# Retention of one decoder block on Trainium2: two halves of the tokens with a state between them, and the decay moved out of the scores

## The chip, the cores and the metric

The kernel runs on one core of one Trainium2 chip. What is measured is the device time of one launch in microseconds (us). The kernel before was run three times: median 1729.63 us, from 1728.58 to 1733.28. One further execution was profiled; it took 1730.48 us, of which 1728.0 us lie between the first and the last instruction (the span). All rows below come from that execution.

## The reference

One layer of a decoder block on 1024 tokens of width 1024, all in float32: half a SwiGLU feed-forward step (inner width 2816), then a mixer, then another half feed-forward step, with an RMS norm ahead of each and one at the end. The mixer projects the normed tokens into 512 columns for a pooling mixer and into queries, keys, values and gates of four heads of 128 columns each. The pooling mixer (trailing means over 2, 4, 8 and 16 tokens, less the token, times a 128x128 matrix per group) is left alone by the change. The heads compute a retention, which the reference writes in chunks; what it amounts to is

```
q, k = rope(q), rope(k) * 128 ** -0.5
gamma[h] = 1 - 2 ** (-5 - h)                     # h = 0..3
o[n] = sum over m <= n of gamma ** (n - m) * (q[n] . k[m]) * v[m]
o = o * rsqrt(mean(o * o) + 1e-6) * gain         # per token and head
b = silu(g) * o
h = h + concat([pooled, b]) @ w_out
```

The sum over m can be split at any token: what lies before the split goes in through one 128x128 matrix per head, the state, which is the sum of k[m] v[m] with the decay up to the split.

## The kernel before

Activations lie with features on the 128 partitions and tokens along the free axis; 1024 tokens (`T`) are worked on in two halves of 512 (`HT`). Each float32 operand is split into two parts of the matmul's input type: ScalarE (ACT) casts the high part, VectorE (DVE) subtracts it from the original and writes the low part (`split`, L78 to L82). A product is then three matmuls, high by high, low by high, high by low, added up in one accumulator in PSUM (`mm3`, L104 to L109). In a profile row such as `ps<-ph,vh` the first operand streams through the array and the second is the one that was loaded as weights. There are eight PSUM banks, all under one tag (`ps`, L73), handed out in turn; a new tile waits until the bank's last reader is done. Weights and read-backs come through three buffers of one tag (`raw`).

The program has three parts: the first feed-forward step (to about 640 us), the mixer (640 to about 1060), the second feed-forward step. The diff touches the mixer alone. There, four projections of the pool run first, then query, key and gate of head 0 (`heads_proj`), the values of heads 0 and 1 (`proj_v`, for two heads at once), and `pool_out`, whose results go to DRAM (`pool_dram`). In `proj_v` the sums in PSUM are split with a factor per token (`scale_split`, L190 to L195): `rcol` holds the norm of each token in the layout with tokens on partitions. The keys and queries pass through `rope` on the way out of PSUM: DVE makes `e`, ACT and GpSimd (POOL) make `f` (L761 to L765), POOL adds them, and `late` splits the sum.

Then come the steps, one for each head, half of the tokens and block of 128 keys. A score tile has keys on the partitions and up to 512 tokens in the free axis. In the first half of a head there are 4 key blocks, with 512, 384, 256 and 128 tokens (what lies above the diagonal is cut off); in the second half 8 key blocks, with 512 tokens five times, then 384, 256, 128. That is 12 steps a head, 48 in all. For each, `scores` makes the tile of the next step on TensorE (PE), DVE multiplies it by a piece of the decay table of the head (`dec`, 1024 columns, L798), and `split` makes `ph` and `pl`. Then comes the fill, then `values` (keys' values by the tile, into an accumulator that runs over the half). The tiles `ph` and `pl` have two buffers each; `p` shares its two (tag `t0`) with `po` of `pool_out`; `f` and the temporary `rs` of the norm share two others (tag `t1`). `dec` has one buffer, which a DMA of 512 KB fills per head, and which it shares with temporaries of the pool.

The fill is work of PE that does not wait for the scores. For heads 0 to 2 it is the projections of the next head: a generator with 24 pieces, each of 6 matmuls of 512 columns (one 128-deep block, three products, two halves). Two pieces stand in each step. For head 3 it is the first part of the output projection (`w_out`), whose accumulators hold two PSUM banks per block of 128 output columns, while `pool_back` reads the pool's results back from DRAM in eight pieces (DMA, cast, subtract). At the end of a half `close` begins: the square of the accumulator for the norm (`ro`), the gain and gate (`y`, L818), and in the steps i+2, i+3, i+4 the pieces of `rstd` (a sum over the partitions by two matmuls with ones, `root`, a Newton step) and the split into `cat`, the input of `w_out`. After the steps the rest of `w_out` runs, with the residual and the next norm.

No table sets the order: the code is written in the order in which each engine's instructions stand, and each engine runs its own in that order.

Of the kernel before, what the change touches and what calls it, by code (L numbers as in the profile page):

```python
# [9 lines left out]
F32 = mybir.dt.float32  # L10
F32R = mybir.dt.float32r
AF = mybir.ActivationFunctionType
ALU = mybir.AluOpType
# [8 lines left out]
NF = FF // P  # L22
NP = NF // 2
# [28 lines left out]
def block(ctx, tc, a):  # L52
# [73 lines left out]
    def rstd(r, n):  # L126

        w = r.shape[-1]
        hi, lo = short("n0", w, F32R), short("n1", w, F32R)
        split(r, hi, lo)  # L130
        yield
        o = ps(w)
        nc.tensor.matmul(o, ones, hi, start=True, stop=False)
        nc.tensor.matmul(o, ones, lo, start=False, stop=True)
        yield from root(o, r, n)

    def root(o, r, n):

        w = r.shape[-1]
        v = short("n2", w)  # L140
        nc.vector.tensor_scalar(out=v, in0=o, scalar1=1.0 / n, scalar2=EPS, op0=ALU.mult, op1=ALU.add)
        yield
        nc.scalar.activation(r, v, AF.Abs_reciprocal_sqrt)
        yield
        s = short("rs", w)
        nc.vector.tensor_tensor(out=s, in0=r, in1=r, op=ALU.mult)  # L146
        nc.vector.tensor_tensor(out=s, in0=s, in1=v, op=ALU.mult)
        nc.vector.tensor_scalar(out=s, in0=s, scalar1=-0.5, scalar2=1.5, op0=ALU.mult, op1=ALU.add)
        nc.vector.tensor_tensor(out=r, in0=r, in1=s, op=ALU.mult)
# [546 lines left out]
    sinr = pool.tile([P, T], F32, name="sinr")  # L696
    r_dram = dp.tile([1, T], F32, name="r_dram", tag="r_dram")
# [32 lines left out]
    def proj_v(pair):  # L730
# [3 lines left out]
        for t0 in (0, 4):  # L734
# [9 lines left out]
            for i, o in enumerate(acc):  # L744
                tb = t0 + i
                scale_split(o, rcol[:, tb:tb + 1], vh[:, tb], vl[:, tb])
# [36 lines left out]
    acc, parts, decs = {}, {}, {}  # L783

    def scores(hd, h, j):

        if hd not in decs:
            decs[hd] = pool.tile([P, T], F32, name="dec", tag="dec", bufs=1)
            nc.sync.dma_start(out=decs[hd], in_=a["decay"][hd])
        q, k = qs[hd][h], ks[hd][0]  # L790
        at = max(0, j * P - h * HT)
        n, off = HT - at, h * HT + at - j * P
        s = ps(n)
        mm3(s, cut(k, slice(None), slice(j * P, j * P + P)), cut(q, slice(None), slice(at, HT)), True, True)
        e = pool.tile([P, HT], F32, name="p", tag="t0", bufs=2)[:, :n]
        ph = pool.tile([P, HT], F32R, name="ph", tag="ph", bufs=2)[:, :n]
        pl = pool.tile([P, HT], F32R, name="pl", tag="pl", bufs=2)[:, :n]
        nc.vector.tensor_tensor(out=e, in0=s, in1=decs[hd][:, off:off + n], op=ALU.mult)  # L798
        split(e, ph, pl)
        parts[hd, h, j] = (ph, pl), at  # L800

    def values(hd, h, j):
        if j == 0:
            acc[hd, h] = ps()
        p, at = parts.pop((hd, h, j))
        vs = slice(hd % 2 * P, hd % 2 * P + P)
        mm3(acc[hd, h][:, at:], cut(vs_of[hd // 2], slice(None), j, vs), p, j == 0, j == 4 * h + 3)

    def close(hd, h):
# [7 lines left out]
        y, ro = (pool.tile([P, HT], F32, name=n, tag=n, bufs=b) for n, b in (("y", 1), ("ro", 2)))  # L817
        nc.scalar.activation(ro, o, AF.Square)  # L818
# [3 lines left out]
        yield from rstd(ro, P)  # L822
# [3 lines left out]
    cats = {}  # L826
# [53 lines left out]
    for n, gi in enumerate((3, 2, 1, 0)):  # L880
# [8 lines left out]
        if n == 1:  # L889
# [5 lines left out]
            nc.sync.dma_start(out=rcol, in_=r_dram.rearrange("o (c p) -> p (o c)", p=P))  # L895
    qs, ks, sgs, vs_of, late_ks = {}, {}, {}, {}, []
# [53 lines left out]
    steps = [(hd, h, j) for hd in range(HEADS) for h in range(2) for j in range(4 * (h + 1))]  # L950
# [4 lines left out]
    for i, (hd, h, j) in enumerate(steps):  # L955
# [10 lines left out]
        n = 2 if hd < 3 or i % 12 < 2 else 1  # L966
# [9 lines left out]
        if j == 4 * h + 3:  # L976
# [116 lines left out]
def _tables(np):  # L1093
# [9 lines left out]
    rel = np.arange(T)[None, :] - np.arange(P)[:, None]  # L1103
    dec = np.exp(lg[:, None, None] * np.maximum(rel, 0)[None]) * (rel >= 0)[None] * float(P) ** -0.5
    invc = np.tile((1.0 / np.arange(1, 17)).astype(f)[None], (P, 1))
    return cos2, sin2, dec.astype(f), invc


def _arrange(np, i):
# [13 lines left out]
    def w2s(w):  # L1123
# [11 lines left out]
    cos2, sin2, dec, invc = _tables(np)  # L1135
# [15 lines left out]
        "decay": c(dec),  # L1151
# [21 lines left out]
```

## Time and profile before

The table shows the profiled execution cut at the borders of the work, by the windows of the trace.

| stretch, us | what runs | length, us | PE busy, us | granted clock |
|---|---|---|---|---|
| 0 to 640 | first feed-forward step | 640 | 625.36 | 0.97 to 1.00 |
| 640 to 776 | projections of pool, head 0, values | 136 | 135.41 | 1.00 |
| 776 to 990 | the steps of the retention | 214 | 203.80 | 0.98 |
| 990 to 1060 | rest of `w_out` | 70 | 70.00 | 1.00 |
| 1060 to 1728 | second feed-forward step | 668 | 650.16 | 0.99 |
| profiled execution | 1730.48 us, span 1728.0 | | 1684.7 (97%) | 0.99 |

The page puts PE at 1684.7 us busy (97% of the span), DVE at 1291.0 (75%), ACT at 847.9 (49%), POOL at 258.3 (15%). PE's matmuls overlap at their ends in the records, so a row's mean duration is longer than the distance from one start to the next. The granted clock is given as a share of full speed (2.4 GHz); the other level is 1.2 GHz, a share of 0.50.

### The profile page before, as it was taken

How to read it: one execution, taken by the hardware profiler on the slowest of the kernel's cores; microseconds unless marked ns; L12 is line 12 of the kernel's file. 1: busy time of each engine (PE TensorE's matmuls, PEld its weight loads, DVE VectorE, ACT ScalarE, POOL GpSimd, SP SyncE). 2: the span in 40 equal slices, each digit the busy share in tenths (PEclk: the TensorE clock that was granted, in tenths of full speed). 3: DMA queues.
4: the chain of work that ended last, by engine and by line, in shares of the span. 5: the costliest groups of instructions: out<-in, count | busy, mean ns of one | idle time of the engine just before them, and what ended most of it. 6: DMA issues, size and time to landing. Idle time of an engine off the chain costs nothing.

```text
span 1728.0 us, 21236 instructions
## 1 busy us (share of the span) xinstructions
PE 1684.7 (97%) x7646; PEld 1395.8 (81%) x7646; DVE 1291.0 (75%) x1933; ACT 847.9 (49%) x1379; POOL 258.3 (15%) x228
## 2 busy tenths in 40 slices
PE   8989999999999999999999999989999999999997
PEld 6778888888888888897887788867888888888886
DVE  4978877787778766836657764878777877788667
ACT  5745545554555443344544443655455545554433
POOL 1022012201220101212202020121022102220200
PEclk9999999999999999999999999999999999999998
DMA  9275467546754653231121254373577457744732
GB/s 280 104 152 107 100 153 153 116 97 148 152 121 106 140 176 116 74 106 36 49 79 60 82 196 152 98 146 88 126 147 144 102 120 147 155 98 113 159 134 98
DMA packets 109210, 212.96 MB, mean 123 GB/s; under 512 B 10929, under 2 KB 12977, under 8 KB 109106
## 3 DMA queue, kind: packets, MB, share of 16 engines
q0 software_dynamic: 45280, 97.53, 29.4%
q1 hardware_dynamic: 62994, 113.54, 20.4%
q8 instruction: 59, 0.97, 0.2%
q10 hardware_dynamic: 832, 0.55, 0.1%
q14 instruction: 45, 0.37, 0.1%
HBM read 114.07 MB, written 94.38 MB: 121 GB/s over the span
## 4 chain that ended last, share of the span: by engine, by line
PE 78%; DVE 8%; issue 7%; DMA 3%; ACT 2%; POOL 1%; SPq 0%; DVEq 0%; ACTq 0%; POOLq 0%
PE ps L109 26%; PE ps L108 26%; PE ps L107 26%; DMA raw<-in_f_w 1%; POOL f L764 1%; DMA raw<-pool_dram 1%; DVE t L82 1%; POOL e L765 1%; DVE pl L82 1%; DMA h_dram<-o 1%; DVE wl L82 1%; DVE rs L146 1%; DVE S L247 0%; DVE y L1080 0%; DVE xs L309 0%
## 5 line engine op out<-in xcount | busy, mean ns | idle before, releaser
L502 POOL DMA_DIRECT2D h_dram<-o x144 | 175.2, 1287 | 867.1 <-DVE o L499 860.9
L81 ACT CAST wh<-raw 128x512 fp32r<-128x512 f32 x275 | 170.4, 620 | 210.7 <-PE ps L109 110.4
L107 PE MATMUL ps<-p,wh 128*128 128x512 f32 x648 | 253.9, 392 | 8.2 <-ACT wh L81 4.9
L82 DVE TENSOR_TENSOR wl<-raw,wh 128x512 fp32r<-128x512 f32 x275 | 186.5, 688 | 95.8 <-ACT wh L81 95.5
L108 PE MATMUL ps<-p,wl 128*128 128x512 f32 x648 | 253.5, 392 | 0.0
L109 PE MATMUL ps<-p,wh 128*128 128x512 f32 x648 | 252.4, 391 | 0.0
L107 PE MATMUL ps<-t,wh 128*128 128x512 f32 x608 | 238.0, 391 | 6.8 <-DVE c L462 5.6
L108 PE MATMUL ps<-t,wl 128*128 128x512 f32 x608 | 237.5, 391 | 0.0
L109 PE MATMUL ps<-t,wh 128*128 128x512 f32 x608 | 237.3, 390 | 0.0
L81 ACT CAST wh<-S 128x512 fp32r<-128x512 f32 x224 | 138.7, 620 | 200.8 <-PE ps L109 132.4
L497 ACT ACTIVATE o<-ps 128x512 f32<-128x512 f32 x288 | 162.4, 598 | 13.0 <-DMA h_dram<-o 4.9
L82 DVE TENSOR_TENSOR wl<-S,wh 128x512 fp32r<-128x512 f32 x224 | 152.3, 686 | 18.4 <-ACT wh L81 17.7
L247 DVE TENSOR_TENSOR S<-raw 128x512 f32<-128x512 f32 x112 | 77.1, 689 | 105.8 <-DMA raw<-in_f_w 60.1
L499 DVE SCALAR_TENSOR_TENSOR o<-ps,o 128x512 f32<-128x512 f32 x216 | 134.0, 681 | 26.1 <-DMA h_dram<-o 17.9
L107 PEld LDWEIGHTS ps<-p,wh 128*128 128x128 f32 x648 | 122.4, 189 | 34.8 <-ACT wh L81 4.9
L108 PEld LDWEIGHTS ps<-p,wl 128*128 128x128 f32 x648 | 122.5, 189 | 25.9 <-DVE wl L82 0.6
L109 PEld LDWEIGHTS ps<-p,wh 128*128 128x128 f32 x648 | 122.4, 189 | 25.5
L107 PEld LDWEIGHTS ps<-t,wh 128*128 128x128 f32 x608 | 114.6, 189 | 32.4 <-DVE c L462 6.4
L109 PEld LDWEIGHTS ps<-t,wh 128*128 128x128 f32 x608 | 114.7, 189 | 24.0
L108 PEld LDWEIGHTS ps<-t,wl 128*128 128x128 f32 x608 | 114.7, 189 | 23.7
L107 PE MATMUL ps<-gt,wh 128*128 128x512 f32 x288 | 112.7, 393 | 0.4 <-ACT o L497 0.4
L108 PE MATMUL ps<-gt,wl 128*128 128x512 f32 x288 | 112.7, 391 | 0.0
(197 smaller groups left out, 3296.3 us busy)
## 6 DMA issues: line engine op xcount, KB each, us to landing
h_dram<-o POOLq DMA_DIRECT2D x144, 512.0 KB, 10.3
raw<-in_f_w SPq DMA_DIRECT2D x176, 256.0 KB, 4.6
raw<-in_f_w2s SPq DMA_DIRECT2D x72, 256.0 KB, 4.7
raw<-in_w_t SPq DMA_DIRECT2D x32, 256.0 KB, 2.7
raw<-in_w_o SPq DMA_DIRECT2D x22, 256.0 KB, 2.9
h_dram<-x SPq DMA_DIRECT2D x8, 512.0 KB, 5.3
raw<-in_f_w2c SPq DMA_DIRECT2D x16, 256.0 KB, 2.9
y<-h_dram SPq DMA_DIRECT2D x16, 256.0 KB, 4.0
```

The source lines that it names most:

```text
L81: nc.scalar.copy(hi, src)
L82: nc.vector.tensor_tensor(out=lo, in0=src, in1=hi.bitcast(F32), op=ALU.subtract)
L107: nc.tensor.matmul(out, lh, rh, start=start, stop=False, skip_group_check=chained)
L108: nc.tensor.matmul(out, ll, rh, start=False, stop=False, skip_group_check=chained)
L109: nc.tensor.matmul(out, lh, rl, start=False, stop=stop, skip_group_check=chained)
L146: nc.vector.tensor_tensor(out=s, in0=r, in1=r, op=ALU.mult)
L247: nc.vector.tensor_tensor(out=self.raw[n, out], in0=self.raw[n, x], in1=self.raw[n, y], op=ALU.add)
L497: nc.scalar.activation(x, o, AF.Copy, scale=half)
L499: nc.vector.scalar_tensor_tensor(out=x, in0=o, scalar=half, in1=x, op0=ALU.mult, op1=ALU.add)
L502: nc.gpsimd.dma_start(out=to, in_=out[q][j // 2], accum_op=ALU.add)
L764: nc.gpsimd.tensor_tensor(out=f, in0=f, in1=sinr[:, sl], op=ALU.mult)
L765: nc.gpsimd.tensor_tensor(out=e, in0=e, in1=f, op=ALU.add)
```

## The change

The decay gamma^(n-m) is taken apart. With n and m in the same half of 512 tokens it is gamma^(511-m') / gamma^(511-n'), where m' and n' count inside of the half. The factor of the key's token (and 128^-0.5) goes into the values when they leave PSUM: `gam` holds it for each head and token, `vscale` is its product with `rcol`, and `proj_v` now scales each head's 128 columns apart. The factor of the token n is not divided out: the sums are too small by it, and the norm of the head that follows removes it, if its 1e-6 is scaled by the factor's square. So `rstd` and `root` take a tile `ep` of 512 columns per head (256 KB by DMA) in place of the constant. A score tile then needs only the causal mask, and only in its first 128 columns, where the diagonal block lies: DVE multiplies those by a 128x128 mask, and the other columns are split straight from PSUM.

The second half of a head no longer runs over the first half's keys. Instead the keys of the first half are turned by a matmul with an identity (`turn`, 4 matmuls of 128 columns for the high part in the first step of a head and 4 for the low part in the second), cast by ACT into `kt`, and multiplied with the values over all four blocks (`summed`, 12 matmuls of 128 columns, in the fourth step). The result, times gamma^512, is split into `st`, and three matmuls of 512 columns (state by queries) open the accumulator of the second half. A head has 8 steps now in place of 12, 32 in all. The 24 pieces of fill stand 4, 3, 3, 3, 4, 3, 3, 3 to a step until they run out; in head 3 there are 2 pieces of `w_out` and 2 read-backs of the pool in a step until they run out.

The diff, cut to its core:

```diff
+DECAY = [(1.0 - 2.0 ** (-5 - i)) ** (T // 2) for i in range(4)]
...
-    def rstd(r, n):
+    def rstd(r, n, eps=EPS):
...
-        nc.vector.tensor_scalar(out=v, in0=o, scalar1=1.0 / n, scalar2=EPS, op0=ALU.mult, op1=ALU.add)
+        if eps is EPS:
+            nc.vector.tensor_scalar(out=v, in0=o, scalar1=1.0 / n, scalar2=EPS, op0=ALU.mult, op1=ALU.add)
+        else:
+            nc.vector.scalar_tensor_tensor(out=v, in0=o, scalar=1.0 / n, in1=eps, op0=ALU.mult, op1=ALU.add)
...
+    gam = pool.tile([P, HEADS, NK], F32, name="gam")
+    vscale = pool.tile([P, HEADS, NK], F32, name="vscale")
+    mask = pool.tile([P, P], F32, name="mask")
+    eye = pool.tile([P, P], F32R, name="eye")
+    nc.scalar.dma_start(out=gam, in_=a["gam"])
+    nc.scalar.dma_start(out=mask, in_=a["mask"][0])
+    raw_eye = pool.tile([P, P], F32, name="raw_eye")
+    nc.scalar.dma_start(out=raw_eye, in_=a["mask"][1])
+    nc.scalar.copy(eye, raw_eye)
...
-                scale_split(o, rcol[:, tb:tb + 1], vh[:, tb], vl[:, tb])
+                for c in range(2):
+                    hs = slice(c * P, c * P + P)
+                    scale_split(o[:, hs], vscale[:, 2 * pair + c, tb:tb + 1], vh[:, tb, hs], vl[:, tb, hs])
...
-    acc, parts, decs = {}, {}, {}
+    acc, parts, keyt, state = {}, {}, {}, {}
     def scores(hd, h, j):
-        if hd not in decs:
-            decs[hd] = pool.tile([P, T], F32, name="dec", tag="dec", bufs=1)
-            nc.sync.dma_start(out=decs[hd], in_=a["decay"][hd])
         q, k = qs[hd][h], ks[hd][0]
-        at = max(0, j * P - h * HT)
-        n, off = HT - at, h * HT + at - j * P
+        at = j * P
+        n = HT - at
         s = ps(n)
-        mm3(s, cut(k, slice(None), slice(j * P, j * P + P)), cut(q, slice(None), slice(at, HT)), True, True)
-        e = pool.tile([P, HT], F32, name="p", tag="t0", bufs=2)[:, :n]
+        mm3(s, blk(k, 4 * h + j), cut(q, slice(None), slice(at, HT)), True, True)
+        e = pool.tile([P, P], F32, name="p", tag="pe", bufs=2)
         ph = pool.tile([P, HT], F32R, name="ph", tag="ph", bufs=2)[:, :n]
         pl = pool.tile([P, HT], F32R, name="pl", tag="pl", bufs=2)[:, :n]
-        nc.vector.tensor_tensor(out=e, in0=s, in1=decs[hd][:, off:off + n], op=ALU.mult)
-        split(e, ph, pl)
+        nc.vector.tensor_tensor(out=e, in0=s[:, :P], in1=mask, op=ALU.mult)
+        if n > P:
+            split(s[:, P:], ph[:, P:], pl[:, P:])
+        split(e, ph[:, :P], pl[:, :P])
         parts[hd, h, j] = (ph, pl), at
+    def turn(hd, i):
+        if i == 0:
+            keyt[hd] = pool.tile([P, 2, 4, P], F32R, name="kt", tag="dec")
+        o = ps()
+        for j in range(4):
+            nc.tensor.matmul(o[:, j * P:j * P + P], blk(ks[hd][0], j)[i], eye, start=True, stop=True)
+        nc.scalar.copy(keyt[hd][:, i].rearrange("p j d -> p (j d)"), o)
+    def summed(hd):
+        o = ps(P)
+        vs = slice(hd % 2 * P, hd % 2 * P + P)
+        for j in range(4):
+            mm3(o, (keyt[hd][:, 0, j], keyt[hd][:, 1, j]), cut(vs_of[hd // 2], slice(None), j, vs), j == 0, j == 3)
+        t = pool.tile([P, 2, P], F32R, name="st", tag="st", bufs=2)
+        scale_split(o, DECAY[hd], t[:, 0], t[:, 1])
+        state[hd] = t[:, 0], t[:, 1]
     def values(hd, h, j):
         if j == 0:
             acc[hd, h] = ps()
+            if h:
+                mm3(acc[hd, h], state.pop(hd), qs[hd][1], True, False)
         p, at = parts.pop((hd, h, j))
         vs = slice(hd % 2 * P, hd % 2 * P + P)
-        mm3(acc[hd, h][:, at:], cut(vs_of[hd // 2], slice(None), j, vs), p, j == 0, j == 4 * h + 3)
+        mm3(acc[hd, h][:, at:], cut(vs_of[hd // 2], slice(None), 4 * h + j, vs), p, j == h == 0, j == 3)
...
+        if h == 0:
+            epst[hd] = pool.tile([P, HT], F32, name="ep", tag="ep", bufs=2)
+            nc.sync.dma_start(out=epst[hd], in_=a["eps"][hd])
...
-        yield from rstd(ro, P)
+        yield from rstd(ro, P, epst[hd])
...
+            nc.vector.tensor_tensor(
+                out=vscale, in0=gam, in1=rcol.unsqueeze(1).to_broadcast([P, HEADS, NK]), op=ALU.mult
+            )
...
-    steps = [(hd, h, j) for hd in range(HEADS) for h in range(2) for j in range(4 * (h + 1))]
+    steps = [(hd, h, j) for hd in range(HEADS) for h in range(2) for j in range(4)]
...
+        if h == 0:
+            if j < 2:
+                turn(hd, j)
+            elif j == 3:
+                summed(hd)
+        n = 2 if hd == 3 else 4 if i % 8 == 0 else 3
...
-        if j == 4 * h + 3:
+        if j == 3:
...
-    rel = np.arange(T)[None, :] - np.arange(P)[:, None]
-    dec = np.exp(lg[:, None, None] * np.maximum(rel, 0)[None]) * (rel >= 0)[None] * float(P) ** -0.5
+    left = HT - 1.0 - np.arange(T) % HT
+    gam = np.exp(lg[:, None] * left) * float(P) ** -0.5
+    gam = gam.astype(f).reshape(HEADS, NK, P).transpose(2, 0, 1)
+    eps = np.tile((EPS * np.exp(2 * lg[:, None] * left[:HT])).astype(f)[:, None], (1, P, 1))
+    mask = np.stack([np.triu(np.ones((P, P), f)), np.eye(P, dtype=f)])
```

Three places in the order of the instructions follow; a name is that of the program's tile, a row with x4 stands for four instructions in a row.

PE, head 0, the first step of the second half, where the first values of that half are added up and the next score tile is begun. Before:

```order
L107 MATMUL ps<-ph,vh 128x512
L108 MATMUL ps<-ph,vl 128x512
L109 MATMUL ps<-pl,vh 128x512
L107 MATMUL ps<-qh,kh 128x512
L108 MATMUL ps<-qh,kl 128x512
L109 MATMUL ps<-ql,kh 128x512
```

Changed:

```order
L108 MATMUL ps<-qh,st 128x512
L109 MATMUL ps<-qh,st 128x512
L110 MATMUL ps<-ql,st 128x512
L108 MATMUL ps<-ph,vh 128x512
L109 MATMUL ps<-ph,vl 128x512
L110 MATMUL ps<-pl,vh 128x512
L108 MATMUL ps<-qh,kh 128x256
L109 MATMUL ps<-qh,kl 128x256
L110 MATMUL ps<-ql,kh 128x256
```

Three matmuls of the queries with the state stand ahead of the values now, and the score tile that follows is the third of four (256 columns) and not the third of eight (512).

DVE, head 3, around the second score tile; `cat` are the two halves of a read-back of the pool, `y` is the gate of head 2's last half, `n` a temporary of its norm. Before:

```order
L798 TENSOR_TENSOR p<-ps,dec 128x384
L82 TENSOR_TENSOR cat_8099<-raw,cat_8099 128x512
L819 SCALAR_TENSOR_TENSOR y<-ps,cols,sg 128x512
L82 TENSOR_TENSOR pl<-p,ph 128x384
L82 TENSOR_TENSOR n_7995<-ro,n_7994 128x512
L798 TENSOR_TENSOR p<-ps,dec 128x256
L82 TENSOR_TENSOR wl<-raw,wh 128x512
L82 TENSOR_TENSOR cat_8099<-raw,cat_8099 128x512
L82 TENSOR_TENSOR pl<-p,ph 128x256
```

Changed:

```order
L793 TENSOR_TENSOR sg<-ps,r 128x512 x2
L83 TENSOR_TENSOR wl<-raw,wh 128x512
L813 TENSOR_TENSOR p<-ps,mask 128x128
L83 TENSOR_TENSOR cat_8134<-raw,cat_8134 128x512 x2
L860 SCALAR_TENSOR_TENSOR y<-ps,cols,sg 128x512
L83 TENSOR_TENSOR pl<-ps,ph 128x256
L83 TENSOR_TENSOR n_8013<-ro,n_8012 128x512
L83 TENSOR_TENSOR pl<-p,ph 128x128
```

Between the mask (before: the decay) of the second tile that is shown and the subtraction that makes its `pl` stand two read-backs and `y`, where one read-back and `y` stood.

PE, head 3, the second step, with the waits that an instruction carries; `ch` and `cl` are the high and low part of a finished head, the input of `w_out`, and DVE_49 and PE_49 are the semaphores of DVE and PE. Before:

```order
L107 MATMUL ps<-qh,kh 128x256
L108 MATMUL ps<-qh,kl 128x256
L109 MATMUL ps<-ql,kh 128x256
L107 MATMUL ps<-ch_6586,wh 128x512 [waits DVE_49]
L108 MATMUL ps<-ch_6586,wl 128x512
L109 MATMUL ps<-cl_6587,wh 128x512
L107 MATMUL ps<-ch_6586,wh 128x512 [waits DVE_49]
L108 MATMUL ps<-ch_6586,wl 128x512
```

Changed:

```order
L108 MATMUL ps<-qh,kh 128x256 [waits DVE_49]
L109 MATMUL ps<-qh,kl 128x256
L110 MATMUL ps<-ql,kh 128x256
L825 MATMUL ps<-eye,kl 128x128 [waits DVE_49]
L825 MATMUL ps<-eye,kl 128x128 x3
L108 MATMUL ps<-ch_6685,wh 128x512 [waits DVE_49,PE_49]
L109 MATMUL ps<-ch_6685,wl 128x512
L110 MATMUL ps<-cl_6686,wh 128x512
L108 MATMUL ps<-ch_6685,wh 128x512 [waits DVE_49,PE_49]
```

The matmuls that turn the low part of the keys (`ps<-eye,kl`) now stand between the score tile and the first piece of `w_out`, take a bank of PSUM of their own, and carry a wait for DVE; so does the score tile.

## Rows read from the trace of the kernel before

**Rows 1.** The page's chain that ended last, share of the span by engine.
```profile
PE 78%; DVE 8%; issue 7%; DMA 3%; ACT 2%; POOL 1%; SPq 0%; DVEq 0%; ACTq 0%; POOLq 0%
```

**Rows 2.** Windows: stretch, us; busy (count) by engine; PEclk; DMA share; GB/s.
```profile
776.00:942.00 166.00, 160.43 (x822) 134.90 (x821) 109.51 (x173) 76.08 (x133) 33.12 (x24) 1.00 0.17 51
942.00:965.00 23.00, 18.43 (x84) 13.98 (x83) 15.78 (x30) 13.48 (x23) 0.74 (x1) 0.99 0.54 166
965.00:972.00 7.00, 6.95 (x20) 5.37 (x20) 5.41 (x12) 2.97 (x6) 0.00 (x0) 0.54 0.17 55
990.00:1060.00 70.00, 70.00 (x310) 57.90 (x310) 44.73 (x64) 29.82 (x45) 11.65 (x16) 1.00 0.54 179
```

**Rows 3.** Waits of PE, 776 to 990: total us, times, longest.
```profile
PE ps L109 <- DVE pl L82: 5.1, 7, 1.3
PE ps L107 <- ACT ph L81: 4.7, 4, 2.9
```

**Rows 4.** Timeline of PE: start, length, what, idle before; stops and low clock.
```profile
938.93 0.44 PE L109 MATMUL ps<-pl,vh 128*128 128x384 f32 x1 [1.35 <-DVE pl L82]
950.95 0.50 PE L107 MATMUL ps<-ph,vh 128*128 128x512 f32 x1 [1.15 <-ACT ph L81]
964.55 0.47 PE L107 MATMUL ps<-ph,vh 128*128 128x128 f32 x1 [2.90 <-ACT ph L81]
966.52 0.63 PE L109 MATMUL ps<-ql,kh 128*128 128x512 f32 x1
966.95 0.63 PE L107 MATMUL ps<-cat,wh 128*128 128x512 f32 x1
```

**Rows 5.** Timeline of PE: matmuls of 512 and 128 columns in a row.
```profile
774.67 0.39 PE L108 MATMUL ps<-um,wl 128*128 128x512 f32 x1
774.90 0.39 PE L109 MATMUL ps<-um,wh 128*128 128x512 f32 x1
...
784.93 0.23 PE L107 MATMUL ps<-qh,kh 128*128 128x128 f32 x1
785.00 0.28 PE L108 MATMUL ps<-qh,kl 128*128 128x128 f32 x1
785.11 0.27 PE L109 MATMUL ps<-ql,kh 128*128 128x128 f32 x1
785.22 0.45 PE L107 MATMUL ps<-um,wh 128*128 128x512 f32 x1
785.51 0.40 PE L108 MATMUL ps<-um,wl 128*128 128x512 f32 x1
```

**Rows 6.** Groups by shape, PE, 770 to 992: busy us, mean ns.
```profile
L109 PE MATMUL ps<-pl,vh 128*128 128x512 f32 x24 | 10.4, 432 | 1.8 <-DVE pl L82 1.8
L109 PE MATMUL ps<-pl,vh 128*128 128x128 f32 x8 | 2.4, 299 | 0.1
```

**Rows 7.** Groups by shape, DVE and ACT, 776 to 990.
```profile
L82 DVE TENSOR_TENSOR pl<-p,ph 128x512 fp32r<-128x512 f32 x24 | 18.3, 763 | 8.9 <-ACT ph L81 8.6
L798 DVE TENSOR_TENSOR p<-ps,dec 128x512 f32<-128x512 f32 x24 | 16.4, 683 | 12.6 <-DMA dec<-in_decay 6.1 <-PE ps L109 4.2 <-DMA pool_dram<-po 2.4
L798 DVE TENSOR_TENSOR p<-ps,dec 128x128 f32<-128x128 f32 x8 | 2.3, 284 | 2.0 <-PE ps L109 2.0
...
L81 ACT CAST ph<-p 128x512 fp32r<-128x512 f32 x24 | 14.9, 619 | 34.1 <-DVE p L798 34.0
L779 ACT ACT_TABLE_LOAD x3 | 3.8, 1283 | 0.1
```

**Rows 8.** Timeline, POOL and DVE side by side.
```profile
812.31 1.61 POOL L765 TENSOR_TENSOR e<-e,f 128x512 f32<-128x512 f32 x1
812.70 1.77 DVE L82 TENSOR_TENSOR pl<-p,ph 128x512 fp32r<-128x512 f32 x1
```

**Rows 9.** Timeline of DVE, the first score tile of head 3.
```profile
949.50 0.69 DVE L798 TENSOR_TENSOR p<-ps,dec 128x512 f32<-128x512 f32 x1 [1.75 <-DMA dec<-in_decay]
```

**Rows 10.** The chain in order of time: a read-back of the pool.
```profile
947.09 3.92 DMA raw<-pool_dram
```

More of the change, by code (lines that the diff above doesn't have):

```diff
@@ L134, in rstd, with root @@
         nc.tensor.matmul(o, ones, lo, start=False, stop=True)
-        yield from root(o, r, n)
-    def root(o, r, n):
+        yield from root(o, r, n, eps)
+    def root(o, r, n, eps=EPS):
         w = r.shape[-1]
         v = short("n2", w)
-        nc.vector.tensor_scalar(out=v, in0=o, scalar1=1.0 / n, scalar2=EPS, op0=ALU.mult, op1=ALU.add)
+        if eps is EPS:
+            nc.vector.tensor_scalar(out=v, in0=o, scalar1=1.0 / n, scalar2=EPS, op0=ALU.mult, op1=ALU.add)
+        else:
+            nc.vector.scalar_tensor_tensor(out=v, in0=o, scalar=1.0 / n, in1=eps, op0=ALU.mult, op1=ALU.add)
         yield
@@ L821, in close @@
         )
-        yield from rstd(ro, P)
+        yield from rstd(ro, P, epst[hd])
         nc.vector.tensor_tensor(out=y, in0=y, in1=ro, op=ALU.mult)
         split(y, *cut(cat[4 + hd], slice(None), sl))
-    cats = {}
+    cats, epst = {}, {}
     def cat_tile(i):
@@ L965, in block @@
             late_ks.pop(0)()
-        n = 2 if hd < 3 or i % 12 < 2 else 1
+        if h == 0:
[4 more added lines that the diff above has]
+        n = 2 if hd == 3 else 4 if i % 8 == 0 else 3
         if hd == 3:
@@ L1102, in _tables @@
     lg = np.log1p(-np.exp2(f(-5.0) - np.arange(HEADS, dtype=f))).astype(f).astype(np.float64)
-    rel = np.arange(T)[None, :] - np.arange(P)[:, None]
-    dec = np.exp(lg[:, None, None] * np.maximum(rel, 0)[None]) * (rel >= 0)[None] * float(P) ** -0.5
+    left = HT - 1.0 - np.arange(T) % HT
[3 more added lines that the diff above has]
+    mask = np.stack([np.triu(np.ones((P, P), f)), np.eye(P, dtype=f)])
     invc = np.tile((1.0 / np.arange(1, 17)).astype(f)[None], (P, 1))
-    return cos2, sin2, dec.astype(f), invc
+    return cos2, sin2, gam, eps, mask, invc
 def _arrange(np, i):
@@ L1134, in _arrange @@
     )
-    cos2, sin2, dec, invc = _tables(np)
+    cos2, sin2, gam, eps, mask, invc = _tables(np)
     return {
@@ L1150, in _arrange @@
         "sin": c(sin2),
-        "decay": c(dec),
+        "gam": c(gam),
+        "eps": c(eps),
+        "mask": c(mask),
         "invc": c(invc),
```

## The prediction

> **What bounds the kernel now.** I read the chain on the page first, then the stretch of the retention in windows, then who waited there, then single rows. The chain that ended last is 78% PE [rows 1]: a microsecond of PE work or of PE standing still that goes is a microsecond of the kernel, unless something else becomes late. The retention's steps run from 776 to 990. In the windows [rows 2] the reader is to see how much of each stretch PE is not busy: 5.6 of the 166 us of heads 0 to 2, 4.6 of 23 at the start of head 3, and then 7 us in which the granted clock is 0.54 on average, so that about 7 x 0.46 = 3.2 us of matmul time are lost. From 990 on PE is full, so what is saved before is not given back there by PE itself. The waits [rows 3] say for whom PE stood still: 11 times, 9.8 us, for DVE's pl and ACT's ph, the two halves of a score tile; seven of these in heads 0 to 2, four in head 3. Before such a stop the pipeline runs out: a 512-column matmul that waited 1.15 counts 0.50 instead of 0.39 [rows 4, 5], and the one before it counted its full 0.39, where the next normally starts after 0.227. A stop thus costs about 0.25 more than its idle time: heads 0 to 2 lose 5.6 + 7 x 0.25 = 7.3, head 3 loses 4.6 + 1.0 + 3.2 of clock = 8.8.
>
> **Matmul work.** Matmuls overlap, so the price is the distance from start to start. At 512 columns it is 0.23 (774.67 to 774.90; over longer runs 0.227). At 128 it is 0.07, 0.11 and 0.11, and the next 512 gives 0.06 back (785.22 to 785.51 is 0.29) [rows 5]; three narrow ones cost 0.29 + 0.06 = 0.35, 0.115 each. Before, the steps have 24 matmuls of 512 in each of six lines (three of scores, three of values), and 8 of 128 [rows 6]. After, each half has only the four blocks of its own half: 8 of 512 in each line, and the state adds 3 of 512 per head. 512 falls from 144 to 48 + 12 = 60; 384 and 256 stay as they are; 128 rises from 48 by 32 (turning the keys) and 48 (summing the state) to 128. That is -84 x 0.227 = -19.1 and +80 x 0.115 = +9.2: -9.9 us. Bounds for the narrow one: 0.07, the smallest distance (sum -13.5), and 0.299, the busy time of the slowest line [rows 6] (sum +4.8). I take 0.115, the row nearest to a run of them.
>
> The Trainium skill, "TensorE: Matmul & The Clock Gate", section "Back-to-back issue gap", gives about 81 ns at 128 columns and 131 at 512 for a sustained stream; by that the work saved would be an estimated 11.0 - 6.5 = 4.5 us. This trace differs in both (115 and 227), and I go by it.
>
> **The score tile's way to PE.** Before: DVE multiplies the tile by the decay (683 ns at 512), ACT casts (619), DVE subtracts (763 on average) [rows 7]. After: DVE masks 128 columns (284), ACT casts the rest straight from PSUM and then the square, DVE subtracts both; from the 128 and 512 rows I estimate 0.5 + 0.3 of ACT and 0.55 + 0.29 of DVE. A full step is 1.45 of DVE before and 1.12 after, and 16 full steps vanish: 16 x 1.45 + 8 x 0.33 = 26 us of DVE less, at a latency that is no longer. More speaks for a shorter wait: pl takes 0.69 where nothing disturbs it, but took 1.77 at 812.70, beside an operation of POOL [rows 8], and 763 on average, while p, which has the same size and reads PSUM, has 683 on average [rows 7]. The new subtraction of the rest reads PSUM as well. The Trainium skill, "SBUF — State Buffer", section "SBUF: two separate sides", calls the ports that these two engines share a lock, for which an instruction of DVE with two SBUF inputs waits; by it 128 columns of a tile stay exposed instead of 512. The rows agree.
>
> There is more cover, too. Between the scores of a step and its values stand the fills of two steps: 2 x 12 matmuls before (5.4 us), 2 x 18 after (8.2) in heads 0 to 2. That is 2.7 more, and of the stops there I saw none longer than the 1.35 at 938.93 [rows 4]. And rs no longer stands right behind a rope in most heads (its buffer comes free when POOL has added e): five times before, twice after. I leave 1.3 of the 7.3: -6.
>
> **Waits that go.** p waited 1.75 for dec's DMA at 949.50 [rows 9], and PE 1.15 for the ph that followed [rows 4]. The mask is loaded once, long before. This is inside the sums of the heads, not beside them.
>
> **Waits that come, in head 3.** All eight read-backs of the pool now stand in the first four steps, two each, and the fifth and sixth both ahead of the second score tile on DVE, where one stood before. w_out holds four of the eight PSUM banks; scores, sum, turn and close take the rest, so a new tile of PE waits until DVE has read an old one out, and a score's bank is now held until pl, not p. The first w_out matmul of the second step waits for y, which stands behind two cat on DVE and, on ACT, behind cat, cat, wh, a table load, two sg and ro: 6 x 0.62 + 1.28 = 5.0 [rows 7], then y 0.7. The fifth read-back is issued when the third has been subtracted and lands up to 3.9 later [rows 10]; at 3.5 that is 3.5 + 5.0 + 0.7 = 9.2. PE has for that time scores 0.5, turn 0.46, twelve fills 2.7, values 0.7, scores 0.35, turn 0.46: 5.2. It idles about 4, against 4.6 before, and I expect the low clock behind it again. Head 3: -0.5. Bounds: nothing idle and no dip (-8.8), and twelve raw loads through three buffers one after the other, 12 x (3.9 + 0.62 + 0.69)/3 = 21 us against 18 of PE work in the four steps, on top of that idle (+3).
>
> **Edits at nothing.** keyt and the state are cast by ACT and split by DVE (0.3 to 0.7 each) with a step's fills, 4.1, until PE reads them. Two vh of 128 columns stand for one of 256, 16 times, under pool_out and the first fills (4 us of PE). ACT's three DMA issues and eye stand ahead of the norm's cast, and vscale on DVE waits for rcol behind three pw. ep is half the bytes of dec and is loaded a head ahead. If one of these covers failed it would cost up to 1; +0.3 for all.
>
> **Sum.** -9.9 - 6 - 0.5 + 0.3 = -16. It is made on one execution of 1730.48 (span 1728.0), 0.05% above the median of 1729.63; from that median, 1713.6.
>
> **The rivals.** (b) Only the arithmetic counts: the waits come back in new places. For it: almost every new bank in head 3 waits for DVE. Against: the cover of 8.2. -9.9: 1719.7. (c) Every wait goes, and with stops no longer than those before 964 (1.15 at most), at which the clock stayed at 0.99 [rows 2, 4], the low clock too: -9.9 - 7.3 - 8 = -25: 1705. For it: dec's wait and its train go; against: the banks. (d) Narrow matmuls cost their 0.299: +4.8 - 6.5 = -1.7: 1728, no change that can be measured. For it: that row; against: the distances. (e) Slower: the bank wait of head 3 comes at each of its steps, and the clock stays low. At 1.2 GHz a 512 starts 0.43 after the last (966.52 to 966.95) [rows 4], 0.2 more. Head 3 has some 100 such matmuls; all of them low cost 20, and four more of idle make 1738. It decides from about 108 such matmuls (16 + 5.2 over 0.2), or as much in idle; the one dip before held fewer than 20 [rows 2], which speaks against it.
>
> **How the numbers follow.** Forecast 0.50 (1709 to 1718), b 0.17, c 0.18, d 0.10, e 0.05. 0.3%, 5.2 us, is what a measurement here can tell from no change. Faster: 0.50 + 0.17 + 0.18 = 0.85; same: d, 0.10; slower: e, 0.05. The range of 8 in 10 takes the forecast, b and most of c: 1703 to 1723.
>
> **What would show it.** The stretch from the first scores to the end of the steps shrinks from 214 to about 198. Matmuls that turn the keys start 0.11 to 0.12 apart; 0.19 or more speaks for d. PE's waits for pl and ph in heads 0 to 2 are under 2 us; if 5 are left, b. In head 3 a wait of 3 to 4 us stands at a ps<-ch matmul for y or pl, with the clock low behind it; no dip means c, a dip over 20 us e. I am wrong if the saving lies outside of this stretch, or if the three parts fall out otherwise and only their sum fits.

## The result, and the profile after

The changed kernel takes 1709.70 us (median of 4 runs, 1708.90 to 1712.24) against 1729.83 for the kernel before (4 runs): a ratio of 0.9883, 95% interval 0.9865 to 0.9901. That is 20.1 us less, where 16 were forecast (1713.6). The profiled execution took 1709.27 us, with a span of 1707.2.

The page of the changed kernel, first busy time (share) and instructions of each engine, then the chain that ended last by engine. PE's share of the chain, 78% in [rows 1], is 84%; DVE has 23.7 us less to do.

```profile
PE 1667.4 (98%) x7642; PEld 1387.5 (81%) x7642; DVE 1267.3 (74%) x1946; ACT 847.0 (50%) x1416; POOL 258.1 (15%) x228
...
PE 84%; issue 6%; DMA 4%; DVE 4%; ACT 1%; POOL 1%; SPq 0%; DVEq 0%; ACTq 0%; POOLq 0%
```

The windows of the stretch in question (columns as in [rows 2]), heads 0 to 2, the start of head 3, and the low clock:

```profile
776.00:926.00 150.00, 150.00 (x824) 131.16 (x823) 89.58 (x178) 74.07 (x156) 33.55 (x25) 1.00 0.18 52
926.00:940.00 14.00, 9.65 (x49) 7.67 (x48) 10.66 (x22) 8.48 (x16) 0.00 (x0) 0.96 0.46 153
940.00:946.00 6.00, 5.10 (x13) 4.04 (x14) 4.38 (x10) 3.88 (x10) 0.00 (x0) 0.53 0.55 172
...
938.85:945.67 6.82, 4.77 (x11) 3.80 (x12) 4.68 (x11) 5.03 (x13) 0.00 (x0) 0.50 0.59 185
```

PE now stands nowhere in heads 0 to 2 (150.00 of 150), where it lost 5.6 of 166 in [rows 2]. The start of head 3 still has 4.35 idle and behind it 0.53 of the clock. The last row takes the stretch in which the low clock (0.50) was granted by itself: it begins inside of the second stop that is shown below, and 4.77 us of it fall on running matmuls. Before, the low clock stood from 964.55 to 971.38, and matmuls ran through all but 0.05 of it:

```profile
964.55:971.38 6.83, 6.78 (x17) 5.33 (x18) 5.83 (x11) 3.42 (x6) 0.00 (x0) 0.50 0.23 74
```

The waits of PE from 776 to 972 (total, times, longest) name what is left; of the eleven for ph and pl of [rows 3] none stands in heads 0 to 2:

```profile
PE ps L108 <- DVE y L860: 3.4, 1, 3.4
PE ps L108 <- ACT cat L82: 1.8, 1, 1.8
```

Single rows of PE: first the end of a score tile and the four matmuls that turn the keys, then the two stops of head 3. The turn takes 0.40 (777.72 to 778.12), so 0.10 each, below the 0.11 of [rows 5]. At 940.90 stands the wait that was forecast, first `w_out` of the second step, for `y`, and behind it rows of 0.63, 0.42 to 0.43 apart, as in [rows 4].

```profile
777.54 0.34 PE L110 MATMUL ps<-ql,kh 128*128 128x384 f32 x1
777.72 0.56 PE L825 MATMUL ps<-eye,kh 128*128 128x128 f32 x4
778.12 0.44 PE L108 MATMUL ps<-um,wh 128*128 128x512 f32 x1
...
935.49 0.47 PE L108 MATMUL ps<-ph,vh 128*128 128x512 f32 x1 [1.81 <-ACT cat L82]
...
940.90 0.77 PE L108 MATMUL ps<-ch,wh 128*128 128x512 f32 x1 [3.44 <-DVE y L860]
941.47 0.63 PE L109 MATMUL ps<-ch,wl 128*128 128x512 f32 x1
```

The groups by shape (busy us, mean ns of one): the sum and the turn on PE, whose records (0.27) are nearly as long as those of [rows 6] (0.30) though they start 0.10 apart; then a full tile on DVE, 283 + 553 + 375 in place of 683 + 763 in [rows 7]. The last averages 375 and not the 284 of its size, since three of the 32 run beside POOL and take 1.2 to 1.4.

```profile
L109 PE MATMUL ps<-vh,kt 128*128 128x128 f32 x16 | 4.4, 275 | 0.0
L825 PE MATMUL ps<-eye,kl 128*128 128x128 f32 x16 | 2.3, 269 | 0.0
...
L813 DVE TENSOR_TENSOR p<-ps,mask 128x128 f32<-128x128 f32 x32 | 9.1, 283 | 7.5 <-PE ps L110 7.5
L83 DVE TENSOR_TENSOR pl<-ps,ph 128x384 fp32r<-128x384 f32 x8 | 4.4, 553 | 0.9 <-ACT ph L82 0.9
L83 DVE TENSOR_TENSOR pl<-p,ph 128x128 fp32r<-128x128 f32 x32 | 12.0, 375 | 0.5 <-ACT ph L82 0.5
```

**Where the time went.** The trace gives the start of each matmul; from the first score tile to the last `w_out` matmul of the mixer it is 280.28 before (776.48 to 1056.76) and 259.79 after (776.52 to 1036.31). So 20.5 of the 20.8 us of span lie there. Added up by kind (from each start to the next, so a stop counts with the matmul that waited before it or for it), heads 0 to 2, until the first score tile of head 3:

| kind | before: count, us | after: count, us |
|---|---|---|
| scores, 512 columns | 54, 12.58 | 18, 4.18 |
| values, 512 columns | 54, 15.79 | 18, 4.08 |
| values, 384 columns | 18, 6.93 | 18, 3.12 |
| norm | 10, 3.27 | 10, 2.30 |
| state, 512 columns | none | 9, 2.04 |
| turn and sum, 128 columns | none | 24, 2.38 and 36, 3.86 |
| all, with fill and the rest | 166.14 | 149.55 |

63 matmuls of 512 less, at 0.2275, are -14.3; the 60 narrow ones cost 6.2 (0.104 each). Work is -8.1, and the other 8.5 of the 16.6 are stops that went, each with the 0.25 or so that it costs beyond its idle time. Head 3 and the rest of `w_out` fell from 114.14 to 110.24, -3.9: a third of 8.1 is work (-2.7), and -1.2 is left for stops and clock.

### The profile page after: what moved, and what is told of

It is laid out like the page before. It is cut to its first block, busy times and chain, and to the rows that moved or that the text cites. A ratio compares the mean times of both kernels' runs of the same rounds, so it can differ in the third digit from the quotient of the medians.

```text
span 1707.2 us, 21302 instructions
## 1 busy us (share of the span) xinstructions
PE 1667.4 (98%) x7642; PEld 1387.5 (81%) x7642; DVE 1267.3 (74%) x1946; ACT 847.0 (50%) x1416; POOL 258.1 (15%) x228
## 3 DMA queue, kind: packets, MB, share of 16 engines
q1 hardware_dynamic: 62994, 112.49, 20.5%
## 4 chain that ended last, share of the span: by engine, by line
PE 84%; issue 6%; DMA 4%; DVE 4%; ACT 1%; POOL 1%; SPq 0%; DVEq 0%; ACTq 0%; POOLq 0%
PE ps L108 28%; PE ps L109 28%; PE ps L110 28%; DMA raw<-in_f_w 1%; DMA h_dram<-o 1%; DVE wl L83 1%; DMA h_dram<-x 0%; DVE S L251 0%; DMA raw<-pool_dram 0%; DMA raw<-in_f_w2s 0%; DMA x<-in_x 0%; DVE y L1129 0%; DVE y L542 0%; POOL e L780 0%; POOL f L779 0%
```

## The experiments

Each kernel is the changed one with the edit shown, timed beside the kernel before in the same job. Time is the median of four or five runs, which lie up to 6 us apart within a kernel; the ratio is against the kernel before. "pl" is the number of PE's waits for DVE's pl until the first `w_out` matmul, and their sum in us; "slow rs" counts the first two operations of the norm's Newton step (0.68 each elsewhere) that took over 1.4 us in that stretch.

| kernel | time, us | ratio (interval) | pl | slow rs |
|---|---|---|---|---|
| before | 1727.91 to 1729.83, by job | 1 | 6, 4.8 | 7 |
| changed | 1709.70 | 0.9883 (0.9865 to 0.9901) | 0 | 2 |
| e1, mask over all columns | 1710.44 | 0.9893 (0.9877 to 0.9908) | 0 | 2 |
| e2, shorter cover | 1710.34 | 0.9891 (0.9878 to 0.9905) | 1, 0.3 | 2 |
| e3, no state, 48 steps | 1721.54 | 0.9953 (0.9940 to 0.9965) | 4, 1.7 | 9 |
| e4, state left out | 1699.20 | 0.9826 (0.9812 to 0.9839) | 2, 0.4 | 2 |
| e5, read-backs from head 2 on | 1710.84 | 0.9895 (0.9878 to 0.9912) | 0 | 2 |
| e6, gate behind close | 1707.66 | 0.9886 (0.9869 to 0.9902) | 0 | 2 |
| e7, both | 1710.20 | 0.9899 (0.9880 to 0.9917) | 1, 0.3 | 2 |
| changed again | 1709.95 | 0.9890 (0.9873 to 0.9906) | 0 | 2 |
| e8, e1 and e2 | 1712.61 | 0.9909 (0.9894 to 0.9923) | 1, 0.3 | 2 |
| e9, read-backs into cat | 1705.16 | 0.9863 (0.9849 to 0.9878) | 0 | 2 |
| e10, e9 and e6 | 1705.88 | 0.9867 (0.9853 to 0.9882) | 0 | 2 |
| e11, e1 with short steps | 1710.15 | 0.9897 (0.9881 to 0.9913) | 2, 0.5 | 4 |

### What the state is worth: e3 and e4

e3 does half of the change (the edit is cut to its core):

```diff
-        at = j * P
+        at = max(0, j * P - h * HT)
...
+        if j < 4 * h:
+            scale_split(s, DECAY[hd], ph, pl)
...
-        n = 2 if hd == 3 else 4 if i % 8 == 0 else 3
+        n = 2 if hd < 3 or i % 12 < 2 else 1
```

> Half of the change: the decay in the values and the norm as in the changed kernel, but no state. 48 steps as before, the first half's tiles of the second half whole, split with the factor gamma^512 straight from PSUM; fill two pieces a step and head 3 as before the change. Matmuls as in the kernel before. Theory 1: work as before (10.8 us more than the changed kernel, 4/3 of the 8.1 measured in heads 0 to 2), cover as before, so that half or more of the 8.4 us of stops stays: 1723 to 1728. Rival A: the work alone, 1719 to 1721.

Measured: 1721.54, between the two. In its trace the stretch to the last `w_out` is 270.3. The decay in the values alone thus takes 10.0 of the 20.5 us, with the matmuls of before, and the state with its 32 steps the other 10.5. PE's waits of e3, 776 to 985 (total, times, longest):

```profile
PE ps L110 <- DVE pl L83: 1.3, 4, 0.3
PE ps L110 <- DVE pl L197: 1.1, 2, 0.5
PE ps L108 <- ACT ph L82: 1.9, 2, 1.1
```

The rows leave out two lines (0.5 for the gate, 0.4 for the norm). In heads 0 to 2 six stops stand (four for pl, 1.7 us, and two of 0.2 for the norm), 2.1 us in all where 5.6 stood. Theory 1 wanted half or more to stay, rival A none: neither is right. Work, cover and number of tiles are those of before here, and nine slow rs stand where seven stood; what differs in heads 0 to 2 is the tile's way through ACT and DVE (and the norm's `ep`), and it took 3.5 of the 5.6.

e4 leaves out `turn`, `summed` and the three matmuls with the state.

> The changed kernel without turn, sum and state matmuls: the second half gets nothing from the first, so that part of the computation is left out. 32 + 48 narrow matmuls and 12 of 512 columns go. Theory 1: 80 x 0.104 + 12 x 0.227 = 11.0 us less, 1698 to 1700, and a bank wait in head 3 that is a little shorter. Rival (narrow matmuls cost the smallest distance, 0.07): 8.3 less, 1701 to 1702. Rival (they cost the busy time of the record, 0.27): 24 less, 1685.

Measured: 1699.20; the stretch in the trace is 248.76, 11.0 less than the changed kernel's 259.79, with about as much standing still (4.8 against 5.25). Theory 1 holds: a narrow matmul between others costs its 0.104, neither 0.07 nor the 0.27 of its record.

### Why the stops of heads 0 to 2 went: e1, e2, e8, e11

e1 sends the whole tile through the mask, as the decay did; e2 deals two pieces of fill ahead of the next score tile; e8 does both; e11 takes e1 and deals the fill 10, 2, 2, ...:

```diff
# e1, e8, e11
-        nc.vector.tensor_tensor(out=e, in0=s[:, :P], in1=mask, op=ALU.mult)
-        if n > P:
-            split(s[:, P:], ph[:, P:], pl[:, P:])
-        split(e, ph[:, :P], pl[:, :P])
+        nc.vector.tensor_tensor(out=e, in0=s, in1=mask[:, :n], op=ALU.mult)
+        split(e, ph, pl)
...
# e2, e8
+        if hd < 3:
+            run(fill, 2)
+            n -= 2
         if i + 1 < len(steps):
...
# e11
+        n = 10 if hd < 3 and i % 8 == 0 else 2
```

> The changed kernel, but the mask is 512 columns wide (ones behind the diagonal block), DVE multiplies the whole tile by it and the whole product is split, as with the decay before. The output is the same. Theory 1 (the stops of heads 0 to 2 went because six pieces of fill, 8.2 us, stand between a tile's scores and its values, where four stood): nothing returns, 1709 to 1711. Rival A (they went because the tile's way is shorter, with 128 columns through DVE's mask and the rest straight from PSUM): 5 to 8 us of waits for pl and ph return, 1715 to 1718.

> The changed kernel, but in heads 0 to 2 two pieces of each step's fill stand ahead of the next score tile and not behind it. Between a tile's scores and its values stand four pieces (24 matmuls, 5.4 us) as before the change, not six; the work is the same. Theory 1: the stops come back in part, PE waits 3 to 7 us for pl and ph in heads 0 to 2, 1713 to 1717. Rival A: no stop, 1709 to 1711.

e1: 1710.44, no stop for a tile in heads 0 to 2: rival A falls. e2: 1710.34. PE waits 0.27 and 0.49 for ph at the last two tiles of head 1, and 1.95 for ph and 0.31 for pl at the last of head 2, where read-backs stand in line: two casts ahead of ph on ACT, a subtraction ahead of the tile's mask on DVE. These 3.0 are at the lower edge of what theory 1 asked for, but most of them are the read-backs', and the time does not show them, since head 3 then waits only 1.3. So route and cover might each be enough alone:

> The changed kernel with both edits of the two experiments that moved nothing: the mask over the whole tile, and two pieces of each step's fill ahead of the next score tile. Theory 2 (either the shorter way of the tile or the longer cover is enough alone, as either left the heads 0 and 1 without stops): now PE waits for pl and ph in heads 0 to 2 again, 4 to 8 us in all, 1714 to 1720. Rival E (the stops went with the 16 tiles and their 26 us of DVE, whatever route and cover): none in heads 0 and 1, 1709 to 1712.

e8: 1712.61 beside 1709.95 for the changed kernel, in ranges of the same job that do not meet (from 1711.06; to 1710.66), though the intervals of their ratios do. But the stops are those of e2 again: 0.56 and 0.49 at the last tiles of head 1, 1.25 and 0.31 at the last of head 2. That is 2.6 where theory 2 wants 4 to 8, and not the none of rival E: neither holds. Without the place behind the read-backs, 1.1 of 5.6 is back. One more condition of before was left, its pace:

> The kernel with the mask over the whole tile, and in heads 0 to 2 the fill dealt unevenly: ten pieces in a head's first step, then two a step. Tile, cover and pace are those of the kernel before: 1.45 us of DVE for a full tile, four pieces between scores and values, a new tile after every 12 matmuls of fill; only the tiles are 8 and not 12 a head. Theory 4 (the stops came where steps followed each other faster than DVE could do a tile and a piece of the norm in close; the change removed them by stretching a step from 12 to 18 matmuls of fill): one or two stops of 0.3 to 1.3 us a head return, 2 to 5 us of waits for pl and ph in heads 0 to 2, 1713 to 1716. Rival (they went with the 16 tiles, wherever the rest stands): none over 0.5 us, 1709 to 1712.

e11: 1710.15, two stops for pl, of 0.23 each, and one of 0.27 and 0.26 for the norm behind each. With tile, cover and pace of before, 1.0 of 5.6 comes back (1.4 with two waits for the state). Theory 4 falls. Its rival, that the stops went with the 16 tiles, has what it asked for: none over 0.5, and 1710.15 in 1709 to 1712. It stands: of the experiments only e3 keeps the 16 tiles, and with the tile's shorter way.

What the traces show beside it is in the last two columns of the table: PE waits for pl where the norm of `close` meets rope. A piece of before, DVE, POOL and PE in order of time (start, length, what, idle before):

```profile
862.68 1.30 POOL L764 TENSOR_TENSOR f<-f,sinr 128x512 f32<-128x512 f32 x1
862.76 1.77 DVE L146 TENSOR_TENSOR rs<-ro 128x512 f32<-128x512 f32 x1 [2.38 <-POOL e L765]
864.05 1.60 POOL L765 TENSOR_TENSOR e<-e,f 128x512 f32<-128x512 f32 x1
864.45 1.62 DVE L82 TENSOR_TENSOR pl<-p,ph 128x384 fp32r<-128x384 f32 x1
866.12 0.45 PE L109 MATMUL ps<-pl,vh 128*128 128x384 f32 x1 [1.31 <-DVE pl L82]
```

`rs` shares its buffer with `f` and waits for POOL. It then runs beside POOL's next operation and takes 1.77 in place of 0.68, and pl, queued behind it and beside the one after, 1.62 in place of 0.55: 2.2 us lost, of which 1.31 are the stop. Each of the six stops for pl of before stands behind such a slow `rs` that began at most 8 us earlier (five of them at most 4.2). In three of the six, with 3.4 of the 4.8 us, pl itself was slow too (1.77, 1.62, 1.62). In e11 two more are slow than in the changed kernel, and two stops are back:

```profile
850.90 1.76 DVE L150 TENSOR_TENSOR rs<-ro 128x512 f32<-128x512 f32 x1 [2.79 <-POOL e L781]
852.19 1.62 POOL L781 TENSOR_TENSOR e<-e,f 128x512 f32<-128x512 f32 x1
852.70 1.67 DVE L151 TENSOR_TENSOR rs<-rs,n 128x512 f32<-128x512 f32 x1
854.29 0.55 DVE L83 TENSOR_TENSOR pl<-p,ph 128x384 fp32r<-128x384 f32 x1
854.89 0.44 PE L110 MATMUL ps<-pl,vh 128*128 128x384 f32 x1 [0.23 <-DVE pl L83]
```

The three kernels with 7, 9 and 4 slow `rs` have 6, 4 and 2 stops for pl, all twelve behind one. The eleven with 2 have five in all, of 0.2 to 0.3, none behind one. What the new dealing of the steps moved is the meeting of `close` and rope. That this meeting is the cause was read from the traces; no run moved it alone, and it does not settle the size: e3 has more slow `rs` than the kernel before, and stops of 2.1 us where 5.6 stood. The meeting, the 16 tiles and the tile's way are not told apart by these runs.

### What holds head 3: e5, e6, e7, e9, e10

The chain in order of time, changed kernel (start, length, what), from the subtraction of the fourth read-back to the `w_out` matmul that waits for `y`:

```profile
932.29 0.61 DVE cat L83
932.92 2.94 DMA raw<-pool_dram
...
936.41 0.61 ACT wh L82
...
937.04 0.96 ACT L794
...
938.34 1.15 ACT sg L794 x2
939.49 0.49 ACT ro L859
...
940.00 0.76 DVE y L860
...
940.90 0.77 PE ps L108
```

The fifth read-back was issued at 931.72, when the third was subtracted; the chain goes by the sixth, issued when the fourth was. Then everything on the list of the prediction follows, 7.85 us from 932.91 to the end of `y`. The forecast of 9.2 counted from the fifth: from 931.72 it is 9.04.

e5 issues four read-backs in head 2 and then one a step:

```diff
...
+        if hd == 2 and i % 8 > 5:
+            run(back, 2)
         if hd == 3:
-            run(back, n)
+            run(back, 1)
```

> The changed kernel, but four of the eight read-backs of the pool stand in the last two steps of head 2 and the other four one to a step in head 3; no more than one stands ahead of a score tile of head 3. Theory 1 (the two stops of head 3, 1.8 and 3.4 us, and the low clock behind, 2.5, come from the read-backs that crowd ACT, DVE and the three raw buffers): both shrink below 1.5 and the clock stays up, 1702 to 1705. Rival C (the bank wait is set by the gate's table load and two activations ahead of the square): the 1.8 goes, the other stays at 2 to 3.5 with its dip, 1706 to 1708. Rival D (the raw buffers hold back the weights of head 2's last fills): 1709 or more.

Measured: 1710.84 (one of the five runs took 1705.80), and PE waits 4.55 us where it waited 5.25, with the longer stop at the other place:

```profile
PE ps L108 <- DVE pl L83: 3.1, 1, 3.1
PE ps L108 <- ACT kt L826: 1.4, 1, 1.4
```

Its chain shows why: the reads still go round the three raw buffers, now with weights between them. And the edit moved less than it says: in the changed kernel four read-backs are already issued by 926.11, as the first score tile of head 3 starts (926.07), though the code puts all eight behind it; in e5 it is five, by 927.86, where that tile starts at 927.20. So e5 hardly tests theory 1.

```profile
927.86 4.40 DMA raw<-pool_dram
...
934.01 0.61 DVE wl L83
...
934.64 3.07 DMA raw<-pool_dram
```

e6 sets the last piece of a head's fill behind the first part of `close`; e7 is e5 and e6.

```diff
-        n = 2 if hd == 3 else 4 if i % 8 == 0 else 3
+        n = 2 if hd == 3 else (4, 3, 3, 3, 3, 3, 3, 1)[i % 8]
```

> The changed kernel, but the last piece of a head's fill, with the gate's two evacuations, stands behind the values and the first part of close: y and its square stand ahead of the table load and the two gate activations. Theory 1: y still waits for the read-backs ahead of it, the stop falls from 3.4 to 2 or more, 1707 to 1710. Rival C: 1.28 + 1.15 us less ahead of y, the stop falls to about 1 and the dip goes, 1704 to 1706.

> Both edits: read-backs from head 2's last steps on, and the gate behind the first part of close. Both theories: no stop over 1 us in head 3 and no dip, 1701 to 1703. If a stop over 2 us is left, another wait stands behind both, and its releaser in the trace names it.

e6: the wait for `y` falls to 0.6, as rival C says, but 1.5 for pl and 0.8 for the gate's evacuation stand beside it; the clock is low for 3.4 us behind them (938.41 to 941.82), and 1707.66 is not told from the changed kernel by its ratio. e7: 1710.20, a miss for both theories: 1.8 for pl at the first values, and the clock low behind it. Moving what stands in line does not help while the line is held up by the buffers. e9 takes these away: the DMA lands in the low half of the cat tile, which is split in place. e10 adds e6.

```diff
-                raw = wp.tile([P, U], F32, name="raw", tag="raw")
+                raw = cat[gi][1][:, sl].bitcast(F32)
                 nc.sync.dma_start(out=raw, in_=pool_dram[gi, :, sl])
```

> The changed kernel again, beside the next three on one chip: 1707 to 1711, with the two stops of head 3 (1.8 and 3.4 us before, give or take 0.5) at the first values and the first w_out of the second step.

> The changed kernel, but each read-back of the pool lands in the low half of its cat tile and is split in place, not through the three raw buffers; all eight DMAs can go out as soon as the projections' input is no longer read. Theory 3 (what sets the stops of head 3 is the round of the three raw buffers: each DMA of 3 to 4 us waits for the buffer that ACT and DVE, in order, free behind score tiles): both stops fall below 1 us, no dip, 1702 to 1705. Rival C (the table load and the gate): the 3.4 stays at 2 or more, 1706 to 1708. Rival F (the casts and subtractions of the read-backs themselves, 8 x 0.62 and 8 x 0.69, crowd the same queues): 1708 to 1711.

> The same with the gate's last piece of fill behind the first part of close. Theory 3: 1 us less at most, 1701 to 1704. Rival C: 2 to 3 us less than the kernel before it in this list. Rival F: no change, 1708 to 1711.

e9: 1705.16 (1704.31 to 1705.94) beside 1709.95 (1709.11 to 1710.66): 4.8 us faster than the changed kernel in the same job, and the fastest here with the whole output. Of the 4.8, the stretch to the last `w_out` has 3.1 (259.10 in the trace of the changed kernel again, 255.97 in e9). One wait of PE is left, and of its chain the end:

```profile
PE ps L108 <- DVE y L860: 2.6, 1, 2.6
```

```profile
934.22 1.20 DVE sg L793 x2
...
936.13 0.68 DVE wl L83
936.82 1.20 DVE cat L83 x2
938.02 0.67 DVE y L860
...
938.83 0.47 PE ps L108
```

The stop at the first values is gone, and no DMA stands in the chain near the end. So theory 3 is right on the first stop and, at its edge, on the time. The second stays at 2.6, as rival C wanted, with a low clock of 3.4 us behind it: `y` now waits behind the gate, a weight and two read-backs on DVE itself, which is in part what rival F names. In e10 two stops of 0.5 and 1.0 take its place, with the clock low behind them, and 1705.88 is no gain: rival C, which forecast 2 to 3 us for that edit, falls.

## Why the prediction came out right, and where not

**Matmul work: right.** -9.9 was forecast; -10.8 measured (4/3 of 8.1). The narrow matmul cost 0.104 and not 0.115 (0.099 in the turn, 0.107 in the sum); e4 confirms the price in the time. The distances of [rows 5] were the rows to go by, and rival d, with the 0.299 of [rows 6], would have missed by 15 us.

**The stops of heads 0 to 2: the term was too small, and its reasons hold in part.** -6 was forecast, -8.5 came: all of the 7.3 went (I left 1.3), and 1.2 more, about half of it with the norm's matmuls (3.27 to 2.30 in the table), whose trains I had not counted. I gave most weight to the shorter way of the tile and to 2.7 us more cover. e3 speaks for the first: without the state and without more cover, it took 3.5 of the 5.6. But once the 16 tiles are gone, neither is needed: with both undone (e8) 1.1 of the 5.6 is back, and 1.6 more behind read-backs. That the tiles themselves are fewer, 26 us of DVE, I counted, but did not weigh as a reason. What I mentioned last, `rs` right behind a rope five times before and twice after, fits where the stops stand in all the traces, not how long they are. The Trainium skill, "SBUF — State Buffer", section "SBUF: two separate sides", tells of a lock between DVE and POOL; the 1.77 of `rs` beside POOL, where 0.68 is its length alone, agrees: the norm meets it, and in the three longest stops the tile's pl as well.

**Head 3: right in kind and place.** A stop of about 4 at a `ps<-ch` matmul of the second step for `y`, and the low clock behind it, were forecast; 3.44 came, at that place, and eleven matmuls at 0.42 or so. What I missed is the other stop, 1.81 at the first values. The view names a cast on ACT as its end, but ph had been cast by then; what ends 0.15 before PE goes on is the subtraction that reads the score tile's bank last. The distance is 0.14 or 0.15 in the traces of changed, changed again, e5, e6 and e7 alike. Rows of the changed kernel (start, length, what):

```profile
932.21 0.69 DVE L83 TENSOR_TENSOR cat<-raw,cat 128x512 fp32r<-128x512 f32 x1
933.41 0.28 DVE L813 TENSOR_TENSOR p<-ps,mask 128x128 f32<-128x128 f32 x1
934.42 0.30 ACT L82 CAST ph<-p 128x128 fp32r<-128x128 f32 x1
934.79 0.55 DVE L83 TENSOR_TENSOR pl<-ps,ph 128x384 fp32r<-128x384 f32 x1
```

So the last 0.7 of the stop is the wait for a bank, held until pl, that the prediction lists and did not price. In e1, where the mask over the whole tile is the bank's last reader, and in e4, where no turn takes a bank, PE goes on 0.05 or 0.06 behind ph. The stop is 1.73 and 2.13 there all the same: most of it is the mask, which stands on DVE at 933.41, behind the subtractions of two read-backs, though the scores were done by 926.92. The stops are together 5.25, against 4.58 before; that the part still gained 1.2 and not 0.5 is for the most part the shorter dip: 4.77 us of matmuls at half speed against 6.78, 1.0 less lost.

**Edits at nothing: right.** The stretch from 640 to 776 has 135.43 of PE after and 135.41 before, so mask, eye, gam and the halved `proj_v` splits cost nothing there; +0.3 was not needed.

**The sum.** -10.8 - 8.5 - 1.2 = -20.5, against -16. The three parts came out in their order, and the error of 4 us is that of the stops, for more than half. Every term erred to the same side, so that none made good for another, and 1709.70 lies at the near end of the forecast's 1709 to 1718.

One sentence ahead of the prediction is too simple: that each engine's instructions stand as the code is written. On DVE they do not. The rows of the order show the mask of the next tile and two `cat` ahead of `y` and of both parts of that tile, though the code writes `y` first, then the tile and then the read-backs. What was worked out from the order rows themselves is not touched by it; that e5 moved less than its edit says is.

## What to carry to other kernels

Count the matmuls at the distance from start to start in the stretch, not at the length of their records: wide ones saved and narrow ones added then price a state in advance to within a microsecond. When a group of stops is to go, look at what stands ahead of the late instruction on its engine, for an operation that takes a multiple of its usual time, before reasoning about cover. An edit of the source moves an instruction only as far as the order in the trace shows it. And a ring of few buffers that serves two streams sets the pace of both; landing one stream in its destination was worth more here than any reordering of the queues.

## What the runs showed of the hardware that was not expected

Rival c rested on stops of at most 1.15 leaving the clock alone (1.35, at 938.93 in [rows 4], did so too). In e3 that holds: five stops of 0.30 to 1.13, spread over 11 us of head 3, and a granted clock of 1.00. In e10 it does not: two stops of 0.48 and 0.98 that end 2 us apart, and the clock is low for as long as behind the single stop of 2.63 in e9. Windows of e3, e10 and e9 (columns as above):

```profile
937.00:985.00 48.00, 44.90 (x209) 36.34 (x209) 34.05 (x69) 24.45 (x49) 0.74 (x1) 1.00 0.31 99
...
934.00:941.11 7.11, 5.52 (x25) 3.87 (x24) 7.11 (x15) 7.05 (x14) 0.00 (x0) 1.00 0.04 11
941.11:944.53 3.42, 3.42 (x9) 2.66 (x9) 2.11 (x6) 1.14 (x4) 0.00 (x0) 0.50 0.42 132
...
939.75:943.16 3.41, 3.41 (x10) 2.63 (x9) 1.87 (x6) 0.95 (x3) 0.00 (x0) 0.50 0.31 77
```

Nor does a longer single stop tell it: in the changed kernel the clock was still up 3.4 us after the stop of 1.81 that ended at 935.49, and fell inside of the next; in e1 it fell 1.6 us after one of 1.73, at 937.15. So in e10 two short stops close together brought as long a low clock as one long stop in e9. And what DVE loses beside POOL is more than a whole operation: 1.77 against 0.68 for the same `rs`.
